# An encoder trunk on one core: gate and up of the FFN by Strassen's scheme, activations kept in memory

## The chip, the cores and the metric

The kernel runs on one core of a Trainium2 chip. The metric is the device time of one execution in microseconds (us), given as the median of three runs; one further execution was profiled, and all rows below come from it. The engines are called PE (TensorE, matmuls), PEld (its weight loads), DVE (VectorE), ACT (ScalarE), POOL (GpSimd) and SP (which issues DMAs).

## What is computed

Two sequences, a prompt of 512 tokens and a sample of 256, go through the same trunk of two layers, width 1024. Each layer is attention with three kinds of heads, then a SwiGLU FFN of width 2816. The change concerns the second half of a layer:

```python
for l in range(DEPTH):
    ...
    x = x + y @ w_out[l]
    h = rms_norm(x, norm_ffn[l])
    gate, up = jnp.split(h @ w_gate_up[l], 2, axis=-1)
    x = x + (jax.nn.silu(gate) * up) @ w_down[l]
```

## The kernel before, in words

**Layout and precision.** Activations lie transposed: 128 of the 1024 features on the partitions in each of `KC` = 8 chunks k, tokens on the free axis. `X[0]` holds the prompt (512 columns), `X[1]` the sample (256). Each fp32 operand is split in two F32R parts, hi (a cast, mostly on ACT) and lo (value minus hi, on DVE or POOL), and each product is three matmuls into the same PSUM bank: hi·hi, hi·lo, lo·hi (`mm3`, L509 to L512). The parts of the normalised activations are `Tph`, `Tpl` (512 columns) and `Tsh`, `Tsl` (256).

**Order.** Nothing is ordered by hand. `Plan` records every operation with a cost, a priority and the buffers it reads and writes, and then lists them one by one: the order on each engine is fixed when the kernel is built, and an engine waits at the head of its list. Buffers belong to kinds ("W", "RAW", "SG", ...), and an operation that needs a buffer of a kind takes the one free first.

**Passage into the FFN.** `emit_out` multiplies the attention output by `w_out` and adds it to `X` (DVE). `norm2` then splits `X` times the norm's gain into the two parts (ACT, then DVE at L544), squares it (L553, L556), splits the sum (L524, L525), adds it over the partitions with a matmul on ones (L530) and takes the reciprocal root as exp(−½ ln) on ACT (L533, L535). The root isn't needed by the matmuls: it scales their results (L1002).

**FFN.** `emit_ffn` goes over the 22 blocks f of 128 FFN columns in parts of 6, 6, 6 and 4 (`FPARTS`). A block's gate and up (u = 0, 1) take, for the prompt and the sample each, 8 chunks × 3 = 24 matmuls, of 512 and of 256 columns: 96 matmuls a block. Its weights are two pieces of 512 KB (`Piece`: DMA into `raw`, cast to `wh` on ACT, difference `wl` on DVE or POOL at L485, L486). Then come the scaling by the root (DVE, L1002), silu (ACT, L1005), gate times up (POOL, L1007), and the two parts of the product (ACT at L1014 and `alo`), which stay in SBUF in buffers of kind "ACT". After the blocks of a part come its 8 output chunks c of the second product, 3 matmuls per block and sequence, added to `X` on DVE. The last part of four blocks goes by 256 tokens.

Of the kernel before, what the change touches and what calls it, by code (L numbers as in the profile page):

```python
# [16 lines left out]
KC = 8  # L17
# [5 lines left out]
FPARTS = (6,6,6,4)  # L23
# [53 lines left out]
class Plan:  # L77
# [4 lines left out]
    FIFO = {"S", "P", "PT", "PTS", "PO", "OT", "OV", "Y", "TB", "BT", "GP", "GS", "W", "RAW", "ACT", "SG", "SQ", "YR", "IV", "YT", "RB", "MC", "CS", "QKG"}  # L82
    GROUP = {"MC": "TB"}
    PSUM = {"D", "S", "PT", "PO", "M", "ANY"}

    def __init__(self):
        self.ops, self.writer, self.readers = [], {}, {}
        self.tiles, self.kinds, self.same, self.unit = [], {}, [], []
        self.floor = -1e9

    def storage(self, kind, bundles):
        lst = self.kinds.setdefault(kind, [])
        for b in bundles:
            ids = []
            for t in b:
# [4 lines left out]
                else:  # L100
                    self.tiles.append(t)
                    ids.append(len(self.tiles) - 1)
                    old = [b for a, b in self.same if a is t]
                    self.unit.append(next(i for i, u in enumerate(self.tiles) if u is old[0]) if old else ids[-1])
            lst.append(tuple(ids))

    def alias(self, new, old):
        for a, b in zip(new, old):
            self.same.append((a, b))
# [42 lines left out]
    def emit(self):  # L152
        clock, dma_free, busy = {}, 0.0, {}
        free = [0.0] * len(self.tiles)
# [19 lines left out]
        def slot_time(o):  # L174
            t, picks, taken = 0.0, [], set()
            for b in o.alloc:
# [3 lines left out]
                for ids in self.kinds[b.kind]:  # L180
                    if any(self.unit[i] in taken for i in ids):
                        continue
                    f = max(free[self.unit[i]] for i in ids)
                    if f < best:
                        best, pick = f, ids
# [3 lines left out]
                taken.update(self.unit[i] for i in pick)  # L189
# [30 lines left out]
        while left:  # L220
# [25 lines left out]
            if o.alloc:  # L246
                for b, ids in zip(o.alloc, slot_time(o)[1]):
# [3 lines left out]
                    for i in ids:  # L251
                        free[self.unit[i]] = INF
# [10 lines left out]
            for b in o.bufs:  # L263
# [4 lines left out]
                if not b.left:  # L268
                    for i in b.slot:
                        free[self.unit[i]] = b.end + self.HOP  # L270
# [15 lines left out]
def trunk(ctx: ExitStack, tc: tile.TileContext, t):  # L286
# [905 lines left out]
```

## Time and profile before

| | us |
|---|---|
| median of three runs | 1836.93 (1836.65 to 1838.26) |
| profiled execution | 1836.76 |
| its span | 1835.0 |
| PE busy | 1792.1 (98%) |
| DVE busy | 934.1 (51%) |
| ACT busy | 765.4 (42%) |
| POOL busy | 479.1 (26%) |

The span is the time between the first and the last instruction of the profiled execution. Busy times of PE come from matmuls that overlap in the pipeline, so the mean duration of one matmul is longer than its distance to the next; distances are read from the timeline.

### The profile page before, as it was taken

The numbers are of one execution on the slowest core, as the hardware profiler recorded it, in microseconds if no ns is written. First come the engines' busy times: TensorE is split into PE (matmuls) and PEld (weight loads), VectorE is DVE, ScalarE is ACT, GpSimd is POOL, SyncE is SP. The second block draws the span as 40 slices with busy tenths as digits, with TensorE's granted clock in tenths as the row PEclk, the third lists the DMA queues.
The fourth block names the chain that finished last, engine by engine and source line by source line (L and its number), as shares of the span: only waits on it lengthen the run. The fifth ranks groups of instructions, "written<-read, shape, count | busy, mean of one in ns | idle before, by whom it ended". The sixth has DMA issues, their size and how long they took to land. (4 is left out here: it accounts for less than half of the span.)

```text
span 1835.0 us, 29851 instructions
## 1 busy us (share of the span) xinstructions
PE 1792.1 (98%) x11984; PEld 1638.9 (89%) x11984; DVE 934.1 (51%) x1835; ACT 765.4 (42%) x1745; POOL 479.1 (26%) x523
## 2 busy tenths in 40 slices
PE   6999999999999999999999999998999999999999
PEld 5999999888888888888999989998888888888889
DVE  7788687762333233333668876768423222222222
ACT  5887586642112112212458756857321221122120
POOL 1564253321101101201215634522230131122031
PEclk9999999999999999999999999999999999999999
DMA  4321110121221222121222202001212112211212
GB/s 154 81 69 36 36 56 26 35 69 50 66 69 55 61 69 69 53 75 58 69 63 71 60 24 65 24 24 36 69 58 80 58 52 71 72 56 54 77 58 81
DMA packets 56891, 110.60 MB, mean 60 GB/s; under 512 B 24496, under 2 KB 29616, under 8 KB 56752
## 3 DMA queue, kind: packets, MB, share of 16 engines
q1 hardware_dynamic: 56752, 108.69, 19.3%
q8 instruction: 94, 1.54, 0.4%
q14 instruction: 45, 0.37, 0.1%
HBM read 105.52 MB, written 3.15 MB: 59 GB/s over the span
## 5 line engine op out<-in xcount | busy, mean ns | idle before, releaser
L485 ACT CAST wh<-raw 128x1024 fp32r<-128x1024 f32 (+1 forms) x186 | 184.4, 992 | 486.1 <-PE ps L511 482.2
L1007 POOL TENSOR_TENSOR p<-p,p 128x512 f32<-128x512 f32 (+1 forms) x88 | 115.0, 1307 | 803.7 <-DVE p L1002 720.7
L486 DVE TENSOR_TENSOR wl<-raw,wh 128x1024 fp32r<-128x1024 f32 (+1 forms) x166 | 194.8, 1174 | 168.5 <-ACT wh L485 168.2
L510 PE MATMUL ps<-Tph,wh 128*128 128x512 f32 x704 | 278.1, 395 | 0.0
L511 PE MATMUL ps<-Tpl,wh 128*128 128x512 f32 x704 | 277.9, 395 | 0.0
L512 PE MATMUL ps<-Tph,wl 128*128 128x512 f32 x704 | 273.9, 389 | 0.0
L511 PE MATMUL ps<-Tsl,wh 128*128 128x256 f32 x704 | 199.1, 283 | 0.0
L512 PE MATMUL ps<-Tsh,wl 128*128 128x256 f32 x704 | 199.2, 283 | 0.0
L510 PE MATMUL ps<-Tsh,wh 128*128 128x256 f32 x704 | 197.5, 281 | 0.0
L1002 DVE TENSOR_TENSOR p<-ps,cs 128x512 f32<-128x512 f32 x88 | 60.4, 686 | 233.6 <-PE ps L512 233.3
L510 PE MATMUL ps<-wh,Tph 128*128 128x256 f32 x512 | 152.7, 298 | 10.0 <-ACT wh L481 8.3
L512 PEld LDWEIGHTS ps<-Tph,wl 128*128 128x128 f32 x704 | 132.4, 188 | 30.1
L511 PE MATMUL ps<-wl,Tph 128*128 128x256 f32 x512 | 147.0, 287 | 5.0 <-DVE wl L482 5.0
L510 PEld LDWEIGHTS ps<-Tph,wh 128*128 128x128 f32 x704 | 133.5, 190 | 17.5
L512 PE MATMUL ps<-wh,Tpl 128*128 128x256 f32 x512 | 147.1, 287 | 0.8 <-DVE Tpl L544 0.8
L511 PEld LDWEIGHTS ps<-Tpl,wh 128*128 128x128 f32 x704 | 133.6, 190 | 15.2
L510 PEld LDWEIGHTS ps<-Tsh,wh 128*128 128x128 f32 x704 | 133.7, 190 | 14.1
L511 PEld LDWEIGHTS ps<-Tsl,wh 128*128 128x128 f32 x704 | 133.7, 190 | 12.8 <-DVE Tsl L544 0.2
L512 PEld LDWEIGHTS ps<-Tsh,wl 128*128 128x128 f32 x704 | 133.7, 190 | 0.0
L510 PE MATMUL ps<-yt,wh 128*128 128x256 f32 (+1 forms) x448 | 132.8, 296 | 0.7 <-DVE xp L963 0.4
L511 PE MATMUL ps<-yt,wh 128*128 128x256 f32 (+1 forms) x448 | 130.6, 291 | 0.0
L512 PE MATMUL ps<-yt,wl 128*128 128x256 f32 (+1 forms) x448 | 130.1, 290 | 0.0
(241 smaller groups left out, 4396.5 us busy)
## 6 DMA issues: line engine op xcount, KB each, us to landing
raw<-in_w_gu SPq DMA_DIRECT2D x88, 512.0 KB, 3.7
raw<-in_w_down SPq DMA_DIRECT2D x48, 384.0 KB, 3.1
raw<-in_w_in SPq DMA_DIRECT2D x32, 512.0 KB, 3.8
raw<-in_w_out SPq DMA_DIRECT2D x16, 512.0 KB, 3.6
raw<-in_w_down SPq DMA_DIRECT2D x8, 512.0 KB, 3.7
tbm<-in_rpb SPq DMA_DIRECT2D x96, 24.0 KB, 2.2
tbm<-in_rpb SPq DMA_DIRECT2D x48, 48.0 KB, 2.4
out_y<-xp SPq DMA_DIRECT2D x8, 256.0 KB, 2.1
```

Of the source, the lines that this page charges most:

```text
L485: act(width, lambda: ACT.copy(self.flat(0), raw[0][:, :width]), r=[raw], w=w[0], prio=prio)
L486: ew(width, lambda E: E.tensor_tensor(self.flat(1), raw[0][:, :width], self.flat(0).bitcast(F32), op=OP.subtract), r=[raw] + w[0], w=w[1], ...
L510: PE.matmul(out, a[0], b[0], start=start, stop=False)
L511: PE.matmul(out, a[0], b[1], start=False, stop=False)
L512: PE.matmul(out, a[1], b[0], start=False, stop=stop)
L1002: dve(n, lambda n=n, u=u, s=s, sg=sg, view=view: DVE.tensor_tensor(sg[u][:, :n], view(u), late[s][0][:, :n], op=OP.mult), r=[accs[u % len( ...
L1007: ew(n, lambda E, n=n, sg=sg: E.tensor_tensor(sg[1][:, :n], sg[0][:, :n], sg[1][:, :n], op=OP.mult), r=[(sg, 0)], w=[(sg, 1), sg], prio=pb ...
```

## The change

**Storage.** All tokens lie in one tile `X` of 768 columns in the order sample, prompt (`OFF`); its halves are the first 384 and the second 384 columns. The parts of the activations, the attention buffers and the new Strassen operands share one large tile `u` of 31 units of 768 columns. Reciprocals in attention take a buffer of another kind, and the squares have one buffer in `norm2`.

**Gate and up.** The activations are seen as a matrix of 2 × 2 blocks: features k < 4 (A) and k ≥ 4 (B) of the first 384 tokens, C and D of the second 384. The weights of a block f are four pieces (256 KB each): features below or above, gate or up. The first `FIRST_F` = 2 blocks of each layer multiply plainly, in matmuls of 384 columns. The other 20 use Strassen's scheme in Winograd's form: seven products of 4 chunks instead of eight, with four sums of weights per block (`sums`) and four sums of activations T1 to T4 per layer, made in `norm2` with their two parts (L646 to L687). Five banks take the results; bank X is added on by three products and copied by ACT after each, and DVE adds the others to the copies.

**Activations through memory.** Gate times up of every block goes to `spill` in DRAM by DMA and is loaded again for the second product, where its two parts are made (`load`). The second product runs behind all 22 blocks, in matmuls of 384 columns, in chunks of 6, 6, 6 and 4 blocks.

```diff
-FPARTS = (6,6,6,4)
+HALF = 384
+OFF = {2: 0, 0: 256, 1: 512}
+NU = 31
+DCH = (6, 6, 6)
+FIRST_F = 2
...
+        def half2(ps, a, z, pr):
...
+            for k in range(4):
...
+                parts(lambda k=k: x(1, k), u["C"], a, z, g0, rx(k), pr)
+                dve(n, lambda D=D, k=k, g1=g1: DVE.tensor_scalar(v(D), x(1, k + 4), g1, None, op0=OP.mult), r=rx(k), w=[D],
+                    prio=pr, fast=True, lock=True, ptr=True)
+                parts(lambda D=D: v(D), u["D"], a, z, None, [D], pr)
+            pr = L + 198.2
+            for k in range(4):
...
+                ew(n, lambda E, E1=E1, k=k: E.tensor_tensor(v(E1), x(1, k), x(0, k), op=OP.subtract), r=rx(k), w=[E1], prio=pr,
+                   on="DVE POOL")
+                dve(n, lambda T2=T2, E1=E1, D=D, g0=g0: DVE.scalar_tensor_tensor(
+                    v(T2), v(E1), g0, v(D), op0=OP.mult, op1=OP.subtract), r=[D, E1, "gcol"], w=[T2], prio=pr, lock=True, ptr=True)
+                parts(lambda T2=T2: v(T2), u["T2"], a, z, None, [T2], pr)
...
+    def sums(srcs, width, prio, after):
...
+        for m, i in (("A11", 0), ("S1", 2), ("A22", 3), ("A12", 1)):
+            dma(128 * 4 * width, lambda m=m, i=i: SP.dma_start(out=raw(m), in_=srcs[i]), w=[q[m]], prio=prio,
+                after=after)
+        for out, x, y, op in (("S3", "S1", "A11", OP.subtract), ("S1", "S1", "A22", OP.add), ("S2", "A11", "S1", OP.subtract),
+                              ("S4", "A12", "S2", OP.add)):
+            ew(width, lambda E, out=out, x=x, y=y, op=op: E.tensor_tensor(raw(out), raw(x), raw(y), op=op), r=[q[x], q[y]],
+               w=[q[out]], prio=prio, on="wadd")
+        for m in b:
+            act(width, lambda m=m: ACT.copy(hi(m), raw(m)), r=[q[m]], w=[(b[m], 0)], prio=prio)
+            ew(width, lambda E, m=m: E.tensor_tensor(lo(m), raw(m), hi(m).bitcast(F32), op=OP.subtract),
+               r=[q[m], (b[m], 0)], w=[(b[m], 1)], prio=prio, on="slo")
...
+    PRODUCTS = (("A11", "A", "X"), ("A12", "B", "Y"), ("S2", "T2", "X"), ("S4", "D", "Z"), ("S3", "T3", "X"), ("A22", "T4", "W"),
+                ("S1", "T1", "V"))
...
+        for f in range(FIRST_F, FC):
+            pr = base + f
+            wb = sums([t["w_gu"][l, f, i] for i in range(4)], 512, pr - 1.5, ends)
...
+            for x, (wn, un, bn) in enumerate(PRODUCTS):
...
+                product(wb[wn], [U[k][un] for k in range(4)], bank[bn], 4, pp, utok, un == "A" or bn != "X", True)
+                pw = pp - 0.05
+                if bn == "X":
+                    i = ("A", "T2", "T3").index(un)
+                    act(HALF, lambda sg=sg, i=i, b=bank["X"]: ACT.copy(sg[i], b[0][:, :HALF]), r=[bank["X"]], w=[(sg, i)],
+                        prio=pw, sbuf=False)
+                else:
+                    for dst, src, op in {"Y": ((0, 0, OP.add),), "Z": ((1, 1, OP.add),), "W": ((3, 2, OP.add),),
+                                         "V": ((1, 1, OP.add), (2, 2, OP.add))}[bn]:
+                        dve(HALF, lambda sg=sg, dst=dst, src=src, op=op, b=bank[bn]: DVE.tensor_tensor(
+                            sg[dst], sg[src], b[0][:, :HALF], op=op), r=[bank[bn], (sg, src)], w=[(sg, dst)], prio=pw)
...
+        def load(f, kind, prio):
...
+                dma(196 << 10, lambda q=q, hs=hs: SP.dma_start(out=q[0][:, :HALF], in_=spill[f][:, hs]), r=[("spill", f, h)],
+                    w=[q], prio=prio)
```

**What it moves.** Three places of layer 0 show the order of before and of the change around the end of norm2; buffers carry their names in the program.

On DVE, where the last split sums of the norm stand (`yt`, the lo part), before:

```order
L556 TENSOR_TENSOR p2_139<-p2_139,p3_140 128x512
L556 TENSOR_TENSOR tbm_144<-tbm_144 128x512
L486 TENSOR_TENSOR wl0_85<-raw0_89,wh0_81 128x1024
L486 TENSOR_TENSOR wl1_86<-raw1_90,wh1_82 128x1024
L553 TENSOR_TENSOR p3_140<-xp_67 128x512
L556 TENSOR_TENSOR p2_139<-p2_139,p3_140 128x512
L525 TENSOR_TENSOR yt2_128<-p0_137,yt2_128 128x256
L525 TENSOR_TENSOR yt1_127<-tbm_144,yt1_127 128x256
L486 TENSOR_TENSOR wl2_87<-raw0_89,wh2_83 128x1024
L525 TENSOR_TENSOR yt0_126<-p2_139,yt0_126 128x256
L486 TENSOR_TENSOR wl3_88<-raw1_90,wh3_84 128x1024
L1002 TENSOR_TENSOR p0_137<-ps3_76,bt0_148 128x256
```

On DVE, the same place in the change (`u` are Strassen operands, `row` the root, `raw`, `ppa` and `w` the first Strassen block's weights):

```order
L649 TENSOR_TENSOR u<-bt,u 128x256
L649 TENSOR_TENSOR u<-p,u 128x256
L652 SCALAR_TENSOR_TENSOR u<-p,gcol,u 128x256
L649 TENSOR_TENSOR u<-bt,u 128x256
L1099 TENSOR_TENSOR y<-ps_77,row 128x384
L561 TENSOR_TENSOR yt<-tbm,yt 128x256
L1099 TENSOR_TENSOR sq<-ps_75,row 128x384
L1099 TENSOR_TENSOR sq<-ps_71,row 128x384
L1099 TENSOR_TENSOR y<-ps_72,row 128x384
L1099 TENSOR_TENSOR y<-ps_74,row 128x384
L1053 TENSOR_TENSOR ppa<-raw 128x512
L1057 TENSOR_TENSOR w<-raw,w 128x512
```

Before, weight lo parts (L486) stand between the norm's operations; now sums of activations stand ahead of the last lo part, and the plain blocks' scalings and the weight sums behind it.

On ACT, where the root and the first silu stand, before:

```order
L524 CAST yt0_126<-p2_139 128x256
L485 CAST wh3_84<-raw1_90 128x1024
L533 ACTIVATE bt0_148<-ps7_80,eps_66 128x256
L535 ACTIVATE bt0_148<-bt0_148 128x256
L533 ACTIVATE cs0_145<-ps7_80,eps_66 128x256
L535 ACTIVATE cs0_145<-cs0_145 128x256
L1005 ACT_TABLE_LOAD
L1005 ACTIVATE p0_137<-p0_137 128x256
L1014 CAST g0b0_96<-p1_138 128x256
```

On ACT in the change:

```order
L560 CAST yt<-tbm 128x256
L569 ACTIVATE row<-ps_78,eps 128x256
L571 ACTIVATE row<-row 128x256
L1082 ACT_TABLE_LOAD
L1082 ACTIVATE y<-y 128x384 x2
L1082 ACTIVATE sq<-sq 128x384
L1082 ACTIVATE y<-y 128x384
L1056 CAST w<-raw 128x512 x2
L1056 CAST w<-ppa 128x512
```

Before, the casts of the weights (L485) stand ahead of the table load of silu; now the root, the table load and the silus of the plain blocks stand ahead of the casts (L1056) of the first Strassen block's weights.

On PE, the last matmul of the norm (L530) before, amid gate and up of the first blocks:

```order
L510 MATMUL ps4_77<-Tph_69,wh3_84 128x512
L511 MATMUL ps4_77<-Tpl_70,wh3_84 128x512
L512 MATMUL ps4_77<-Tph_69,wl3_88 128x512
L530 MATMUL ps7_80<-yt1_127,ones_136 128x256 x2
L510 MATMUL ps5_78<-Tsh_71,wh0_81 128x256
L511 MATMUL ps5_78<-Tsl_72,wh0_81 128x256
L512 MATMUL ps5_78<-Tsh_71,wl0_85 128x256
```

On PE in the change (L566 is the same matmul; `ps3` is the bank of a plain block, `ps5` the first Strassen product's):

```order
L546 MATMUL ps3_74<-u_79,w_80 128x384
L547 MATMUL ps3_74<-u_79,w_80 128x384
L548 MATMUL ps3_74<-u_79,w_80 128x384
L566 MATMUL ps7_78<-yt_81,ones_70 128x256 x2
L546 MATMUL ps5_76<-u_79,w_80 128x384
L547 MATMUL ps5_76<-u_79,w_80 128x384
L548 MATMUL ps5_76<-u_79,w_80 128x384
```

It now stands between the last plain product and the first product of the first Strassen block.

## Rows read from the trace of the kernel before

**Rows 1.** Page, part 1: busy us (share of the span) x instructions, by engine.

```profile
PE 1792.1 (98%) x11984; PEld 1638.9 (89%) x11984; DVE 934.1 (51%) x1835; ACT 765.4 (42%) x1745; POOL 479.1 (26%) x523
```

**Rows 2.** Windows: us from:to, length, busy (x) by engine, PE clock, DMA share, GB/s.

```profile
0.00:26.00 26.00, 9.89 (x40) 8.91 (x40) 21.14 (x46) 17.34 (x37) 5.31 (x6) 1.00 0.64 217
26.00:60.00 34.00, 32.51 (x258) 31.99 (x258) 22.11 (x54) 20.28 (x59) 11.09 (x22) 0.95 0.31 83
360.00:395.00 35.00, 34.53 (x225) 31.52 (x225) 28.76 (x48) 20.86 (x41) 10.73 (x9) 1.00 0.20 61
410.00:900.00 490.00, 490.00 (x2837) 431.30 (x2837) 161.66 (x236) 103.86 (x149) 62.28 (x45) 1.00 0.21 64
1262.00:1300.00 38.00, 37.98 (x260) 35.20 (x259) 33.17 (x64) 22.56 (x45) 2.30 (x3) 1.00 0.13 43
```

**Rows 3.** Waits of PE in 360 to 395: us in total, times, longest.

```profile
PE ps L510 <- DVE xp L963: 0.4, 1, 0.4
```

**Rows 4.** Timeline of PE in the second product: start, duration, engine, line, operation.

```profile
699.96 0.40 PE L510 MATMUL ps<-Tph,wh 128*128 128x512 f32 x1
...
701.35 0.28 PE L510 MATMUL ps<-Tsh,wh 128*128 128x256 f32 x1
...
702.06 0.40 PE L510 MATMUL ps<-Tph,wh 128*128 128x512 f32 x1
```

**Rows 5.** Timeline of ACT, the gate's silus of two blocks.

```profile
425.92 0.94 ACT L1005 ACTIVATE p<-p 128x256 f32<-128x256 f32 x2
...
442.76 0.94 ACT L1005 ACTIVATE p<-p 128x256 f32<-128x256 f32 x2
```

**Rows 6.** Timeline of DVE in the passage of layer 0.

```profile
361.02 1.69 DVE L544 SCALAR_TENSOR_TENSOR Tpl<-xp,gcol,Tph 128x256 fp32r<-128x256 f32 x4
...
365.66 0.41 DVE L939 TENSOR_TENSOR yt<-y,yt 128x256 fp32r<-128x256 f32 x1
365.99 1.27 DVE L544 SCALAR_TENSOR_TENSOR Tpl<-xp,gcol,Tph 128x256 fp32r<-128x256 f32 x3
...
377.52 0.68 DVE L553 TENSOR_TENSOR p<-xp 128x512 f32<-128x512 f32 x1
378.12 0.68 DVE L553 TENSOR_TENSOR tbm<-xs 128x512 f32<-128x512 f32 x1
```

**Rows 7.** DVE by form: operation x count | busy, mean ns | idle before.

```profile
L674 DVE TENSOR_TENSOR ppa<-ps,qkg 128x384 f32<-128x384 f32 x48 | 26.4, 550 | 5.3 <-ACT ppa L673 5.0
...
L859 DVE TENSOR_TENSOR rp<-ps,rp 128x128 fp32r<-128x128 f32 x24 | 6.8, 281 | 0.3 <-ACT rp L858 0.2
```

**Rows 8.** ACT by form, same columns.

```profile
L1014 ACT CAST g0a<-p 128x512 fp32r<-128x512 f32 x18 | 11.1, 618 | 92.2 <-POOL p L1007 92.2
...
L715 ACT CAST stk<-ppa 128x384 fp32r<-128x384 f32 x48 | 24.5, 510 | 19.0 <-PE ps L728 6.6 <-DVE ppa L710 6.4 <-POOL ppa L710 5.2
...
L533 ACT ACTIVATE rb<-ps,eps 128x256 f32<-128x256 f32 x18 | 8.5, 474 | 4.5 <-PE ps L530 2.5 <-PE ps L519 1.8
L535 ACT ACTIVATE rb<-rb 128x256 f32<-128x256 f32 x18 | 7.5, 418 | 0.3
...
L1005 ACT ACT_TABLE_LOAD x2 | 2.6, 1283 | 0.0
```

**Rows 9.** POOL by form, same columns.

```profile
L716 POOL TENSOR_TENSOR stk<-ppa,stk 128x384 fp32r<-128x384 f32 x16 | 16.3, 1016 | 21.6 <-ACT stk L715 21.6
...
L1007 POOL TENSOR_TENSOR p<-p,p 128x256 f32<-128x256 f32 x44 | 58.2, 1322 | 271.2 <-DVE p L1002 201.4 <-ACT p L1005 69.8
L1007 POOL TENSOR_TENSOR p<-p,p 128x512 f32<-128x512 f32 x44 | 56.9, 1293 | 532.5 <-DVE p L1002 519.3 <-ACT wh L485 13.2
...
L906 POOL TENSOR_TENSOR yr<-y 128x256 f32<-128x256 f32 x30 | 22.1, 738 | 52.0 <-DVE y L903 52.0
```

**Rows 10.** DMA issues: operation x count, KB each, us to landing.

```profile
raw<-in_w_gu SPq DMA_DIRECT2D x88, 512.0 KB, 3.7
...
out_y<-xp SPq DMA_DIRECT2D x8, 256.0 KB, 2.1
```

More of the change, by code (lines that the diff above doesn't have):

```diff
@@ L102, in storage, with atom, part, named @@
                     ids.append(len(self.tiles) - 1)
-                    old = [b for a, b in self.same if a is t]
-                    self.unit.append(next(i for i, u in enumerate(self.tiles) if u is old[0]) if old else ids[-1])
+                    at = [a for z, a in self.same if z is t]
+                    self.unit.append(at[0] if at else (self.atom(None, 0),))
             lst.append(tuple(ids))
-    def alias(self, new, old):
-        for a, b in zip(new, old):
-            self.same.append((a, b))
+    def atom(self, key, i):
+        if key is None or (key, i) not in self.grid:
+            self.natoms += 1
+            if key is None:
+                return self.natoms - 1
+            self.grid[key, i] = self.natoms - 1
+        return self.grid[key, i]
+    def part(self, whole, key, lo, hi):
+        t = whole[:, lo:hi]
+        return self.named(t, key, lo, hi)
+    def named(self, t, key, lo, hi):
+        self.same.append((t, tuple(self.atom(key, i) for i in range(lo // 128, -(-hi // 128)))))
+        return t
     def buf(self, kind):
@@ L180, in slot_time @@
                 for ids in self.kinds[b.kind]:
[L181 removed]
+                    if taken and any(z in taken for i in ids for z in unit[i]):
                         continue
[L183 removed]
+                    f = max([free[z] for i in ids for z in unit[i]])
                     if f < best:
@@ L251, in emit @@
                     for i in ids:
-                        free[self.unit[i]] = INF
+                        for z in unit[i]:
+                            free[z] = INF
             o.start = s
@@ L269, in emit @@
                     for i in b.slot:
-                        free[self.unit[i]] = b.end + self.HOP
+                        for z in unit[i]:
+                            free[z] = b.end + self.HOP
             for z in o.opts:
@@ L920, in emit_out @@
             q = sq[m, p]
-            late = K["lo"] and m == TURN[-1]
-            rb = P.buf("RBL" if late else "RB")
+            rb = P.buf("RB")
             root([(lambda q=q: q[0], q)], wd, po, K["om"] if m == TURN[-1] else 0, rb, lambda rb=rb: rb[0], rb)
@@ new lines, in trunk, with product, mm @@
+    PRODUCTS = (("A11", "A", "X"), ("A12", "B", "Y"), ("S2", "T2", "X"), ("S4", "D", "Z"), ("S3", "T3", "X"), ("A22", "T4", "W"),
+                ("S1", "T1", "V"))
+    def product(wb, ub, bank, n, prio, tok, first, last, open_=True):
+        for kk in range(0, n, 2):
+            ks = list(range(kk, min(kk + 2, n)))
+            def mm(ks=ks):
+                for k in ks:
+                    w = [wb[0][:, z * 512 + k * 128:z * 512 + k * 128 + 128] for z in range(2)]
+                    u = [ub[k][0][:, z * HALF:z * HALF + HALF] for z in range(2)]
+                    mm3(bank[0][:, :HALF], w, u, first and k == 0, last and k == n - 1, open_ and not first)
+            pe(3 * len(ks) * (HALF / 2400.0 + 0.014), mm, r=[(wb, 0), (wb, 1)] + [x for k in ks for x in tok(ub[k])], w=[bank], prio=prio)
@@ L1094, in trunk @@
         P.floor = L + 90
-        ends, late = norm2(l, [L + K["nf"] + p + (K["n2"] if p == 2 else 0.0) for p in range(3)])
+        ends, row, U = norm2(l, [L + K["nf"] + p + (K["n2"] if p == 2 else 0.0) for p in range(3)])
         P.floor = -1e9
-        last = emit_ffn(l, L + 200, ends, late)
+        last = emit_ffn(l, L + 200, ends, row, U)
         if l + 1 < DEPTH:
```

525 lines of the change are left out of this document (268 added, 257 removed).

## The prediction

> **What bounds the kernel now.** I read the shares of busy time first, then stretches of the span, then TensorE's own rows, then the rows that price the work of the other engines. TensorE is busy 98% of the span, VectorE 51%, ScalarE 42%, GpSimd 26% [rows 1]. The reader should see in the stretches that this is not an average over good and bad: in 490 us of FFN TensorE stands 0.00 us and VectorE works a third of the time [rows 2]. So the FFN's time is its matmul columns. The places where TensorE does wait are the first 26 us (9.89 busy [rows 2]) and bits of attention; 1835.0 − 1792.1 [rows 1] leaves 42.9 us of waiting, 16.1 of it in those 26 us. The passage from attention to the FFN, which the change rewrites, is nearly free of waits today: 0.47 us stand in 35 in layer 0, with one wait of 0.4, and 0.02 in 38 in layer 1 [rows 2, 3]. But VectorE is the engine that works hardest there, 28.76 of 35 and 33.17 of 38 [rows 2].
>
> My sum starts from the profiled execution, 1836.76 us, 0.2 us under the median of the three runs. No change can be told from a change under 0.2%, about 3.7 us.
>
> **Price of the matmuls.** Six 512-column matmuls start within 1.39 us (699.96 to 701.35), six 256-column ones within 0.71 (to 702.06) [rows 4]: 0.2317 and 0.1183 each. A block of 128 FFN columns has 48 of either: 48 × 0.35 = 16.8 us. Two silus of neighbouring blocks start 425.92 and 442.76, 16.84 apart, which agrees [rows 5]. The change's 384-column matmul isn't in the trace. 512 + 256 columns cost 0.35, so two of 384 cost the same if time goes by columns: 0.175. Scaled from the narrow row alone it would be 1.5 × 0.1183 = 0.1775, from the wide one 0.75 × 0.2317 = 0.1738. I take 0.175, since the pair holds the same columns, and keep those bounds.
>
> **Strassen blocks.** Seven products × 4 contraction chunks × 3 = 84 matmuls of 384, 84 × 0.175 = 14.7 us against 16.8. Saved: 2.1 us in each of 20 blocks in each of 2 layers, **−84**. By the bounds of the price it is 40 × (16.8 − 14.91) = −76 to 40 × (16.8 − 14.6) = −88. The two plain blocks of a layer have 192 matmuls of 384, 33.6 us, as before. The second product has the same columns (3 × 0.2317 + 3 × 0.1183 = 1.05 before, 6 × 0.175 = 1.05 after, per FFN block and output chunk), and its last part stays: 0.
>
> **The passage into the FFN.** The new norm2 makes, besides the two parts of the scaled activations, four Strassen sums of them and their two parts, and VectorE does most of it. By the order of the changed program in layer 0, from VectorE's row of the first add of the sample's attention output (L1026) to the last lo part of the root (L561, the excerpt), there stand 28 operations of 512 columns between tensors, 31 scalar-tensor ones of 256 and 28 of 128, 27 tensor-tensor ones of 256 and 16 of 128, 8 tensor-scalar ones and 4 of 384 out of PSUM. Prices, start to start: 0.60 for 512 (377.52 to 378.12), (1.69 − 0.08)/4 = 0.40 for a scalar-tensor one of 256, 0.33 for a tensor-tensor one of 256 (365.66 to 365.99) [rows 6]; 0.47 for 384 out of PSUM (550 ns less the overlap of 0.08) and 0.20 for 128 (281 less the same) [rows 7]. The scalar-tensor one of 128 and the tensor-scalar ones aren't shown: the first lies between 0.20 (the tensor-tensor one of 128) and 0.40 (its own of 256), I take 0.26 and so −1.7 to +3.9 us on the stretch; for the second 0.2 to 0.3. Sum: 16.8 + 12.4 + 7.3 + 9.0 + 3.2 + 1.9 + 1.9 = 52.5 us. TensorE's rows in the same stretch are 108 matmuls of 256 (12.8 us), the 192 of the plain blocks (33.6) and the roots' (0.9): 47.3. VectorE is **5.2 us late**, and nothing later on TensorE's queue is free of it: in the excerpt of TensorE the last root matmul stands between the last plain product and the first Strassen product. Before, it stood amid gate and up products, with 512-column work on both sides.
>
> Behind that root there is a chain. The root's Ln and Exp (0.47 and 0.42), the load of silu's table (1.28), four silus of 384 (about 0.42 each by the 0.51 of a 384 cast less overlap), and only then on ScalarE's queue the casts of the first Strassen weights (0.54 start to start, from 0.62), and VectorE's lo part (0.60) [rows 6, 8]: the excerpt of ScalarE shows this order. With the root's matmuls (0.3) that is 5.3 us in which TensorE's next product has no weights. Before, the casts of the weight pieces stand ahead of the table load in ScalarE's order. So layer 0 stands 5.2 + 5.3, about **11 us**. In layer 1 the stretch has 33 operations of 512, three more of 256 and four more of 384: 58.5 us against 12.8 + 204 × 0.175 + 0.9 = 49.4 up to the product that first needs the last of them: **9 us**. Both could be zero if GpSimd and ScalarE take the work sooner than I count, and both could be 15 if VectorE must wait for ScalarE's hi parts ahead of each lo part.
>
> **The clock after a gap.** After the first 26 us, in which TensorE was busy 38%, the next 34 us ran at a mean granted clock of 0.95, everywhere else in the FFN at 1.00 [rows 2]. 0.95 of 34 is 1.7 us lost, that is 3.4 us at 1.2 GHz. Two gaps of about 10 us may each bring that: **+3**, between 0 and 3.4. By the Trainium skill ("TensorE: Matmul & The Clock Gate", "What's actually happening") the array's default is the throttled state, half rate, and activity releases it; the row agrees, and by the rule the two gaps cost as much as by the row if they are unbroken, nothing if scattered.
>
> **Steady Strassen blocks.** Per block of 14.7 us VectorE has 4 sums of weights and 6.1 of 7 lo parts at 0.60, 5 reads of PSUM at 0.47 and 3.1 scalings at 0.5: 9.9 us. ScalarE has 7 casts (0.62) and 5 other operations of 384 (0.51): 6.9. GpSimd has 2.2 products and 0.9 scalings of 384 (1.02 each) and 0.9 lo parts of 512 (1.29): 4.3 [rows 6 to 9]. All are below 14.7, so they hide behind TensorE. Weights and banks are awaited 80 to 100 matmuls after the work that frees them stands in order; the closest is the bank that three products add on, whose copy by ScalarE has 10 matmuls, 1.75 us, of cover, against a copy of 0.5 behind at most one cast of 0.62. I take **+1** for all blocks, with 0 and 24 (0.6 a block) as ends. Transfers: four of 256 KB a block and two spills replace two of 512 KB (3.7 us each) [rows 10]; the second product's reloads stand 18 to 27 matmuls (3 to 5 us) ahead. At a DMA share of 0.21 [rows 2] I cost them at nothing; uncovered, a reload is about 2.1 us (a 256 KB store [rows 10]).
>
> **Storage.** One buffer fewer in attention (reciprocals shared, squares single) and weights in other places: 0, between −3 and +3, a tenth of the 26.8 us that TensorE waits outside the start.
>
> Sum: 1836.8 − 84 + 11 + 9 + 3 + 1 = 1776.8, so **1777 us**.
>
> **Rivals.**
> *The passage is covered.* The row for it: before, TensorE waits 0.4 us there with VectorE at 82% [rows 2, 3], and two plain blocks give 33.6 us of cover. Against it: the counts above. Time: 1836.8 − 84 + 0 to 4 = 1753 to 1757.
> *The blocks are bound in part.* Each block stands 0.25 to 0.6 us at the shared bank or at a late lo part: 40 of them cost 10 to 24, so 1787 to 1801. For it: scalings and lo parts are queued in order on VectorE among PSUM reads; against it: the 5 us of slack.
> *The other side: VectorE and GpSimd lengthen each other until a block is theirs.* GpSimd's 256-column product takes 1322 ns among VectorE's work, another 256-column operation of its, in attention, 738 [rows 9]. If not one of their operations could overlap, a block would take 9.9 + 4.3 = 14.2, still under 14.7. It decides from a block of 14.7 + (84 − 24)/40 = 16.2, when each operation is also 14% longer than its row; a block of 16.8 would give 1837 + 24 = about 1861. The Trainium skill ("SBUF — State Buffer", "Who interferes with whom") says that a VectorE operation with two inputs in SBUF and a GpSimd operation that reads SBUF hold a shared pair of ports exclusively. By that rule only 7.6 + 4.3 = 11.9 us of a block exclude each other, which is no bound either; the two rows agree that the engines hinder each other.
>
> **How the numbers follow.** Forecast 0.66, passage covered 0.12, blocks bound in part 0.14, other side 0.08. The forecast's own bounds (76 to 88 saved, stalls 10 to 28, clock 0 to 3, storage ±3) give 1756 to 1796 with all at one end; taking in most of the first two rivals makes 1753 to 1804. Faster 0.89 (all but the last case and a little for the unforeseen), same 0.03, slower 0.08.
>
> **What would show it.** Right: silus of neighbouring Strassen blocks 14.7 us apart; TensorE free of waits in the blocks; a gap of about 10 us in each layer ahead of the first Strassen product, released by VectorE or by the weights' cast; a granted clock under 1 just behind it. Wrong: 384-column matmuls far from 0.175 us, which moves the sum by 1 us for each 0.0003; blocks of 15.3 or more, with waits for ScalarE's bank copies; passages without a gap; GpSimd rows much longer than 1.3 us.

## The result, and the profile after

The changed kernel takes 1783.11 us (median of four, 1781.19 to 1784.08) against 1837.56 for the kernel before: a ratio of 0.9703, 95% interval 0.9686 to 0.9719, so 54.5 us less. The forecast was 1777, its range 1753 to 1804. The profiled execution has a span of 1782.3 us, 52.7 less than that of before.

The shares of busy time of the changed kernel, to be read beside [rows 1]:

```profile
PE 1712.3 (96%) x11504; PEld 1682.5 (94%) x11504; DVE 1310.0 (74%) x2511; ACT 917.7 (51%) x2151; POOL 542.0 (30%) x577
```

TensorE lost 79.8 us of busy time, but its share fell: 1782.3 − 1712.3 leaves 70.0 us of waiting, 27.1 more than before. VectorE went from 934.1 to 1310.0 us.

ScalarE's timeline in the Strassen blocks of the changed kernel, the first silu of a block and the first of the next, which answer to [rows 5]:

```profile
601.85 0.53 ACT L1082 ACTIVATE y<-y 128x384 f32<-128x384 f32 x1 [1.28 <-DVE y L1127]
...
616.40 0.53 ACT L1082 ACTIVATE y<-y 128x384 f32<-128x384 f32 x1 [1.28 <-DVE y L1127]
```

A block takes 616.40 − 601.85 = 14.55 us (five blocks from there take 72.80, 14.56 each), against 16.8: a 384-column matmul is 14.56 / 84 = 0.1733 us.

TensorE's waits in the changed kernel over the whole span (us in total, times, longest), some of the rows that answer to [rows 3]; layer 0's waits in front of the Strassen blocks follow piece by piece below:

```profile
PE ps L548 <- DVE w L1057: 9.7, 2, 9.4
...
PE ps L956 <- DVE y L971: 4.2, 2, 2.1
...
PE ps L546 <- DVE x L1026: 3.8, 4, 1.0
...
PE ps L546 <- ACT y L1115: 0.8, 1, 0.8
```

and four of its stretches, with the columns of [rows 2]:

```profile
350.00:400.00 50.00, 46.82 (x310) 46.12 (x311) 45.12 (x115) 30.15 (x81) 14.19 (x17) 0.97 0.05 17
395.00:411.20 16.20, 15.89 (x91) 15.26 (x89) 16.16 (x46) 9.16 (x25) 2.48 (x2) 1.00 0.00 2
400.00:430.00 30.00, 21.17 (x99) 19.43 (x98) 27.15 (x54) 16.29 (x34) 7.78 (x6) 0.77 0.24 82
430.00:800.00 370.00, 369.22 (x2129) 368.69 (x2129) 282.15 (x426) 152.73 (x285) 103.61 (x81) 1.00 0.36 111
```

The reader sees two gaps: in layer 0, 21.17 of 30 us busy at a mean clock of 0.77; then blocks that wait for 0.78 us in 370. Ahead of the gap it is VectorE that is full: 16.16 of 16.2 us, where ScalarE is busy 9.16. In layer 1 there is one wait of 9.4 for the lo part of a weight (L1057). TensorE's timeline shows the gap of layer 0 piece by piece:

```profile
413.90 0.58 PE L566 MATMUL ps<-yt,ones 128*128 128x256 f32 x1 [3.00 <-ACT yt L560]
415.36 0.58 PE L566 MATMUL ps<-yt,ones 128*128 128x256 f32 x1 [0.88 <-DVE yt L561]
420.54 0.69 PE L546 MATMUL ps<-u,w 128*128 128x384 f32 x1 [4.59 <-ACT w L1056]
...
421.90 0.69 PE L548 MATMUL ps<-u,w 128*128 128x384 f32 x1 [0.36 <-DVE w L1057]
```

3.00 and 0.88 us are lost ahead of the two last root matmuls, 4.59 and 0.36 ahead of the first Strassen weights: 8.8 us.

### The profile page after: what moved, and what is told of

Same layout as the page of the kernel before. It is cut to its first block, busy times and chain, and to the rows that moved or that the text cites. A ratio compares the mean times of both kernels' runs of the same rounds, so it can differ in the third digit from the quotient of the medians.

```text
span 1782.3 us, 30961 instructions
## 1 busy us (share of the span) xinstructions
PE 1712.3 (96%) x11504; PEld 1682.5 (94%) x11504; DVE 1310.0 (74%) x2511; ACT 917.7 (51%) x2151; POOL 542.0 (30%) x577
## 4 chain that ended last, share of the span: by engine, by line
PE 81%; DVE 10%; ACT 7%; issue 1%; DMA 1%; SPq 0%; DVEq 0%
PE ps L546 24%; PE ps L547 24%; PE ps L548 24%; PE ps L956 3%; PE ps L934 2%; PE ps L875 2%; ACT p L922 1%; ACT u L941 1%; DVE u L652 1%; ACT w L521 1%; DVE w L522 1%; PE ps L807 1%; DVE u L649 1%; DVE x L1026 1%; DVE u L942 1%
## 5 line engine op out<-in xcount | busy, mean ns | idle before, releaser
L548 PE MATMUL ps<-u,w 128*128 128x384 f32 (+1 forms) x1684 | 559.7, 332 | 9.7 <-DVE w L1057 9.7
L546 PE MATMUL ps<-u,w 128*128 128x384 f32 (+1 forms) x1684 | 559.8, 332 | 5.4 <-ACT w L1056 4.6
L547 PE MATMUL ps<-u,w 128*128 128x384 f32 (+1 forms) x1684 | 559.3, 332 | 0.0
L548 PEld LDWEIGHTS ps<-u,w 128*128 128x128 f32 x1684 | 317.8, 189 | 10.6 <-DVE w L1057 10.6
L546 PEld LDWEIGHTS ps<-u,w 128*128 128x128 f32 x1684 | 317.7, 189 | 6.5 <-ACT w L1056 4.9
L547 PEld LDWEIGHTS ps<-u,w 128*128 128x128 f32 x1684 | 317.8, 189 | 0.0
L546 PE MATMUL ps<-w,u 128*128 128x256 f32 x768 | 228.8, 298 | 12.5 <-ACT w L521 9.3
L547 PE MATMUL ps<-w,u 128*128 128x256 f32 x768 | 219.1, 285 | 5.3 <-DVE w L522 5.3
L548 PE MATMUL ps<-w,u 128*128 128x256 f32 x768 | 219.2, 285 | 0.0
L521 ACT CAST w<-raw 128x1024 fp32r<-128x1024 f32 (+2 forms) x102 | 94.9, 932 | 209.2 <-PE ps L547 187.8
L546 PEld LDWEIGHTS ps<-w,u 128*128 128x128 f32 x768 | 148.6, 193 | 14.6 <-ACT w L521 9.3
L547 PEld LDWEIGHTS ps<-w,u 128*128 128x128 f32 x768 | 148.9, 194 | 6.3 <-DVE w L522 5.6
L548 PEld LDWEIGHTS ps<-w,u 128*128 128x128 f32 x768 | 148.5, 193 | 0.0
L546 PE MATMUL ps<-yt,w 128*128 128x256 f32 x392 | 114.3, 291 | 3.9 <-DVE x L1026 3.8
L522 DVE TENSOR_TENSOR w<-raw,w 128x768 fp32r<-128x768 f32 (+2 forms) x87 | 97.2, 1119 | 24.8 <-ACT w L521 17.8
L956 PE MATMUL ps<-u 128*128 128x256 f32 (+1 forms) x592 | 105.6, 296 | 9.4 <-DVE u L942 4.6
L547 PE MATMUL ps<-yt,w 128*128 128x256 f32 x392 | 111.9, 286 | 0.2 <-DVE yt L1012 0.2
L548 PE MATMUL ps<-yt,w 128*128 128x256 f32 x392 | 111.6, 285 | 0.0
L942 DVE TENSOR_TENSOR u<-ps,u 128x512 fp32r<-128x512 f32 (+1 forms) x160 | 97.2, 625 | 18.2 <-ACT u L941 17.4
L875 PE MATMUL ps<-u 128*128 128x256 f32 (+1 forms) x384 | 94.8, 349 | 7.8 <-DVE sm L919 3.9
L956 PEld LDWEIGHTS ps<-u 128*128 128x128 f32 x592 | 84.7, 194 | 14.6 <-DVE u L942 7.1
```

The costliest lines, as they stand in the source:

```text
L521: act(n, lambda hs=hs: ACT.copy(self.flat(0)[:, hs], raw[0][:, hs]), r=[raw], w=[(b, 0) + z], prio=prio)
L522: ew(n, lambda E, hs=hs: E.tensor_tensor(self.flat(1)[:, hs], raw[0][:, hs], self.flat(0)[:, hs].bitcast(F32), op=OP.subtract), r=[raw, (b ...
L546: PE.matmul(out, a[0], b[0], start=start, stop=False, skip_group_check=on)
L547: PE.matmul(out, a[0], b[1], start=False, stop=False, skip_group_check=on)
L548: PE.matmul(out, a[1], b[0], start=False, stop=stop, skip_group_check=on)
L875: PE.matmul(S[0][:, :nk], q, kk[:, k0:k0 + nk], start=i == 0, stop=i == 1)
```

## The experiments

Each time is a median with its ratio to the kernel before on the same chip, and its interval.

**One more plain block per layer.**

```diff
-FIRST_F = 2
+FIRST_F = 3
...
-        for h in range(2):
-            for f in range(FIRST_F):
-                sg, pp = sgs[f], base - 1 + 0.4 * h + 0.2 * f
+        for h, f in [(0, 0), (0, 1), (1, 0), (1, 1)] + [(h, f) for f in range(2, FIRST_F) for h in range(2)]:
+            if True:
+                sg, pp = sgs[f], base - 1 + 0.4 * h + 0.2 * f + (0.8 if f > 1 else 0.0)
```

> A third plain block per layer ahead of the Strassen blocks, nothing else. Theory (the two gaps of 8.9 and 9.4 us are VectorE's and ScalarE's lateness after the sums of activations, with 5.5 us of half clock behind them): 16.6 us more cover closes both, so -18.3 - 5.5 + 2 x (16.64 - 14.56) = about -19.6, 1763 us, and no gap. Rival chain (root, table load, silus and the casts of the first Strassen weights hang together wherever the first Strassen block stands): the 5 us of layer 0 stay, behind the third block, and layer 1's may too: 1770 to 1787. Rival banks (the third block's own weights come late, since its casts queue behind norm2's): a new wait ahead of the third block, 1775 or more.

Measured: 1771.53 us, 0.9636 (0.9621 to 0.9650), 11.6 us less than the changed kernel. TensorE's two longest waits of this kernel from 380 to 440 us, in layer 0:

```profile
PE ps L546 <- DVE y L1099: 3.6, 1, 3.6
PE ps L546 <- ACT y L1115: 2.0, 1, 2.0
```

And its waits from 1250 to 1330 us, in layer 1:

```profile
PE ps L546 <- DVE y L1099: 1.6, 1, 1.6
PE ps L546 <- ACT y L1115: 1.4, 1, 1.4
```

Both gaps for weights are gone, also the 4.6 us behind the root, so the chain was not tied to the Strassen block: it only had no cover. In their place stand waits that no theory named: the third block's accumulators need banks, and a bank is held until VectorE has scaled it by the root (L1099), which is still late; and the first Strassen blocks wait for ScalarE's copy of bank X (L1115). They are 3.6 + 2.0 + 1.6 + 1.4 = 8.6 us, about what is missing between the 11.6 us that came back and 19.6. By its time alone the run would fit the chain rival's 1770 to 1787; the waits which that rival needs are gone.

**The sums of activations left out.**

```diff
             pr = L + 198.2
-            for k in range(4):
+            for k in range(0):
                 u, D = U[k], Ds[k]
...
-                product(wb[wn], [U[k][un] for k in range(4)], bank[bn], 4, pp, utok, un == "A" or bn != "X", True)
+                product(wb[wn], [U[k][{"T1": "B", "T2": "C", "T3": "D", "T4": "A"}.get(un, un)] for k in range(4)], bank[bn], 4, pp, utok, un == "A" or bn != "X", True)
```

> The sums of activations T1 to T4 aren't made; their products take B, C, D, A in their place, so the matmuls stay and norm2 loses about 19 us of VectorE work a layer. Theory: layer 1's gap of 9.4 goes, layer 0's shrinks by at least the 3.9 us ahead of the root, and the clock's 5.5 with them: 1760 to 1767. Rival chain: the gaps stay where the casts of the first Strassen weights are late: 1778 to 1783.

Measured: 1766.18 us, 0.9606 (0.9592 to 0.9620). In layer 0's passage these waits are left, besides one of 0.2 us:

```profile
PE ps L546 <- DVE x L1026: 1.9, 2, 1.0
PE ps L548 <- DVE w L1057: 0.3, 1, 0.3
```

Without the sums the gaps are 0.3 us. The chain of root, table load, silus and casts is still there, in the same form, and costs nothing when it starts earlier; the rival falls. The sums also gave ScalarE and GpSimd work, so this run alone doesn't say which engine was late; the row from 395 to 411.2 us does, where VectorE is full and ScalarE isn't. The gaps are VectorE's lateness.

**All blocks plain.**

```diff
-FIRST_F = 2
+FIRST_F = 22
...
```

> All 22 blocks plain (no Strassen product, no sums), with everything else of the change: one tile of tokens, 384 columns, activations through memory, the second product behind all blocks. Theory (these cost nothing, and 20 blocks by Strassen save 2.08 us each against plain ones of 16.64): 1783 + 40 x 2.08 - 18.3 (gaps) - 5.5 (clock) - 3.8 (bank waits of the output product) = 1838.6, the time of the kernel before. Rival (the storage and the way through memory cost something that the Strassen blocks hide in my account): 1845 or more.

Measured: 1842.15 us, 1.0023 (1.0013 to 1.0033), 3.5 us over the sum, under the rival's 1845. The first silus of two blocks are 16.64 us apart:

```profile
507.42 0.53 ACT L1082 ACTIVATE y<-y 128x384 f32<-128x384 f32 x1 [0.15 <-DVE y L1099]
...
524.06 0.53 ACT L1082 ACTIVATE sq<-sq 128x384 f32<-128x384 f32 x1 [0.16 <-DVE sq L1099]
```

So the rest of the change is dearer than the plain kernel by some 4 us, though 384 columns save 0.16 us a block. The Strassen blocks are worth 1842.15 − 1783.11 = 59.0 us, of 40 × 2.08 = 83.2: 24 us were given back, 19 of them in the two gaps and the waits behind them. TensorE's waits for L971 and L1026 stand in this kernel too, 4.4 and 3.8 us, so they belong to the rest of the change and not to the Strassen blocks.

**Matmuls without use in the gaps, twice.** The first run put layer 1's in the wrong place; the second moved them. In the diff the last two lines are the second run against the first.

```diff
...
+                for _ in range(warm if ks[0] == 0 else 0):
+                    PE.matmul(bank[0][:, :HALF], ones, ub[0][0][:, :HALF], start=True, stop=True)
...
-                        warm=(22, 46)[l] if (f, x) == (FIRST_F, 0) else 0)
+                        warm=(24, 46)[l] if (f, x) == (FIRST_F, l) else 0)
```

> Matmuls without use fill the gaps: 32 of 128 columns ahead of layer 0's last root matmul, 22 of 384 behind it, 46 of 384 ahead of the first Strassen product in layer 1. Theory: the gaps end when they ended before, but the clock stays at 2.4 GHz in and behind them, which gives back the 6.6 and 4.4 us at half rate behind the gaps, 5.5 us in all: 1777.6, granted clock 1.00 in the 20 us after each gap. Rival (what runs slowly behind the gap is the late weights, not the clock): 1783, no change.

> As the run before with matmuls without use, but in layer 1 they stand where the gap is (46 ahead of the second product of the first Strassen block), 24 and 32 in layer 0 as before. Theory: both gaps end where they ended, the clock stays at 2.4 GHz behind both: 1783 - 5.5 = 1777.6. If the first run's 1785.8 was right for another reason than the misplaced 46 (8 us ahead of the gap), this one is no faster either: 1783 to 1786.

Measured: 1785.76 us, 0.9715 (0.9699 to 0.9730), with 4.8 us of layer 1's gap left; and 1781.70, 0.9694 (0.9679 to 0.9708). Windows of the changed kernel in and behind the two gaps (PE busy first, the clock third from the end):

```profile
412.00:416.00 4.00, 1.16 (x2) 0.58 (x2) 3.31 (x9) 1.65 (x6) 0.00 (x0) 0.65 0.00 0
416.00:420.00 4.00, 0.00 (x0) 0.00 (x0) 2.55 (x5) 3.94 (x8) 1.19 (x1) 0.50 0.00 0
420.00:424.00 4.00, 3.11 (x9) 2.60 (x10) 3.45 (x3) 0.73 (x2) 4.00 (x4) 0.50 0.61 193
424.00:428.00 4.00, 4.00 (x17) 4.00 (x17) 3.89 (x7) 3.45 (x7) 0.11 (x1) 0.65 0.68 229
1300.00:1304.00 4.00, 1.11 (x3) 1.11 (x4) 3.96 (x9) 1.57 (x4) 0.00 (x0) 0.50 0.16 57
1304.00:1308.00 4.00, 4.00 (x15) 4.00 (x15) 4.00 (x8) 3.31 (x7) 0.00 (x0) 0.57 0.54 161
```

and of the second run:

```profile
416.00:420.00 4.00, 3.56 (x21) 3.56 (x22) 2.57 (x7) 3.07 (x6) 0.29 (x1) 1.00 0.00 0
420.00:424.00 4.00, 2.83 (x15) 2.19 (x15) 2.96 (x3) 1.38 (x4) 4.00 (x4) 1.00 0.44 93
424.00:428.00 4.00, 3.19 (x16) 2.34 (x15) 3.88 (x6) 2.79 (x6) 1.04 (x1) 1.00 0.77 252
1300.00:1304.00 4.00, 2.58 (x15) 2.26 (x14) 3.96 (x8) 1.48 (x4) 0.00 (x0) 1.00 0.07 25
1304.00:1308.00 4.00, 4.00 (x24) 3.85 (x24) 4.00 (x7) 2.90 (x6) 0.00 (x0) 1.00 0.84 234
```

The clock does follow the gap: filled, it stays at 2.4 GHz, where the changed kernel runs behind both gaps at 1.2 GHz. The windows give the rate lost in the changed kernel as the clock below 1 times TensorE's busy time: 0.4 + 1.6 + 1.4 in layer 0 and 0.6 + 1.7 in layer 1, some 5.6 us. But the medians are only 1.4 us apart, which is within the spread of the runs. In the traces 1.1 us came back in layer 0 (from the last plain matmul to a silu deep in the blocks, 410.56 to 616.40 us against 411.64 to 616.36) and 1.3 in layer 1 (from its first silu, 1282.05 to 1493.93 against 1281.14 to 1491.73).

Behind layer 0's gap TensorE is busy 3.19 of 4 us instead of 4.00: at full rate it stands still for operands that aren't ready. One is a weight whose cast waits for its load (ScalarE's timeline of the second run):

```profile
424.85 0.62 ACT L1059 CAST w<-raw 128x512 fp32r<-128x512 f32 x1 [3.47 <-DMA raw<-in_w_gu]
```

In the changed kernel that load is issued at 420.79 us, right behind the first spill in SyncE's queue; the spill waits 30.4 us for GpSimd's product, and so for the root. Behind layer 1's gap TensorE is busy 4.00 us in both, and does 24 matmuls instead of 15. So the clock cost less than its lost rate, 1.4 us by the medians and 2.4 by the traces, in layer 0 since the engine that it slowed would have waited.

**A buffer of its own for attention's reciprocals.**

```diff
...
-            inv, iv = P.buf("M"), P.buf("YR")
+            inv, iv = P.buf("M"), P.buf("IV")
```

> The reciprocals of attention get a buffer of their own again (64 more columns in the row's tile). The change's attention has 5.7 us more waits and 4.7 us more half clock than before. Theory that the shared buffer makes them: they go, 1773 to 1777. Rival (they come from the new order, VectorE taking norm2's work for the sample ahead of attention's last adds): 1781 to 1785.

Measured: 1786.03 us, 0.9718 (0.9703 to 0.9732). TensorE's waits for L971 and L1026 fell from 8.0 to 4.5 us, but all its waiting is 70 us as before: others took their place. So a buffer of its own gave no time back; whether the shared one has a part in those waits isn't settled.

**VectorE's slack in a block.** S4, one of the four sums of weights, is computed 5, 10 and 2 times.

```diff
-            ew(width, lambda E, out=out, x=x, y=y, op=op: E.tensor_tensor(raw(out), raw(x), raw(y), op=op), r=[q[x], q[y]],
+            ew(width, lambda E, out=out, x=x, y=y, op=op: [E.tensor_tensor(raw(out), raw(x), raw(y), op=op)
+                                                                for _ in range(5 if out == "S4" else 1)], r=[q[x], q[y]],
```

> In each Strassen block one sum of weights (S4) is computed five times instead of once, with the same result: 2.4 us more VectorE work a block, order unchanged. VectorE is busy 282 of 370 us in the blocks of layer 0, 11.1 us of 14.56. Theory (blocks are TensorE's until VectorE fills them): 13.5 of 14.56, so only the first block of each layer is later, +2 to +5: 1785 to 1788. Rival (blocks are bound in part already, VectorE's queue in order): 0.5 us or more a block, 1803 or more.

> The same sum ten times: 5.4 us more VectorE work a block. Theory: 11.1 + 5.4 = 16.5 us of VectorE in a block of 14.56, VectorE becomes the bound: 40 x 1.9 = +78, 1855 to 1870, slower than the kernel before; the slack of a block lies between the two runs. Rival (VectorE's busy time holds waits that shrink): under 1830.

> S4 computed twice instead of once in each Strassen block, same result, order unchanged: one more VectorE operation of 512, 0.6 to 0.9 us a block. The run with four more lost 2.84 us a block though VectorE was not full. Theory now: VectorE's queue holds the row scaling, the silu waits for it at the head of ScalarE's queue, and the copy of the shared bank X stands behind the silu; the block has about the 2.2 us of slack in which VectorE is idle in the changed kernel, so one operation fits: 1783 to 1787. Rival (no slack at all, each operation costs its 0.7 us a block): 1808 to 1813.

Measured: 1896.68 us, 1.0312 (1.0295 to 1.0329); 2090.28, 1.1372 (1.1355 to 1.1389); 1788.48, 0.9732 (0.9716 to 0.9748). My theory of the first two fell: four more operations cost 113.6 us, 2.84 a block, while VectorE isn't full. The window 500 to 700 us of the changed kernel:

```profile
500.00:700.00 200.00, 200.00 (x1156) 200.00 (x1155) 164.34 (x242) 87.84 (x168) 70.05 (x54) 1.00 0.35 103
```

The same window with S4 computed 2 times:

```profile
500.00:700.00 200.00, 200.00 (x1156) 200.00 (x1155) 173.28 (x259) 85.09 (x169) 71.49 (x55) 1.00 0.35 103
```

Four steady blocks with S4 computed 5 times:

```profile
612.72:680.25 67.53, 59.36 (x336) 58.08 (x336) 61.22 (x89) 24.53 (x49) 20.95 (x17) 1.00 0.29 86
```

And 10 times, from 500 to 700 us:

```profile
500.00:700.00 200.00, 146.01 (x726) 143.13 (x725) 168.82 (x248) 53.55 (x105) 46.61 (x34) 0.85 0.22 66
```

The expectations had the added work too small: one of the sums takes 0.91 us there (4.56 for five, below), not 0.60. With four more, VectorE is busy 61.22 / 4 = 15.3 us a block, against 164.34 / 200 × 14.56 = 12.0 in the changed kernel. That is over 14.56, but by VectorE alone a block would be 15.3; it is 67.53 / 4 = 16.88, and VectorE is idle for 1.6 of it. With nine more it is idle for 31 of 200 us.

The run of 5 times shows why, first in VectorE's timeline:

```profile
606.15 4.56 DVE L1053 TENSOR_TENSOR raw<-tbm,ppa 128x512 f32<-128x512 f32 x5
610.63 1.48 DVE L1121 TENSOR_TENSOR y<-y,ps 128x384 f32<-128x384 f32 x3
612.02 1.94 DVE L1128 TENSOR_TENSOR y<-y,row 128x384 f32<-128x384 f32 x2
```

In ScalarE's at the same time:

```profile
612.72 0.52 ACT L1083 ACTIVATE y<-y 128x384 f32<-128x384 f32 x1 [5.24 <-DVE y L1128]
613.15 0.60 ACT L1057 CAST w<-p 128x512 fp32r<-128x512 f32 x1
613.66 0.47 ACT L1116 COPY y<-ps 128x384 f32<-128x384 f32 x1
```

And in TensorE's:

```profile
614.18 0.45 PE L546 MATMUL ps<-u,w 128*128 128x384 f32 x1 [2.04 <-ACT y L1116]
```

The five sums take 4.56 us; the PSUM reads and the row scaling (L1128) wait behind them; the silu waits 5.24 us for the scaling at the head of ScalarE's queue (1.28 in the changed kernel); the copy of the shared bank X (L1116) stands behind it and a cast; and TensorE waits 2.04 us for that copy in every one of these blocks. With one more operation the steady blocks don't change (TensorE 200.00 of 200 busy); the kernel is 5.4 us longer, of which waits for bank X in the first blocks of each layer, up from 0.8 to 4.6 us, are most. The slack of a block is thus between the 0.65 us that VectorE's load rose here (173.28 − 164.34 in 200 us) and the 3.3 of the run with four more.

**GpSimd's FFN work on VectorE.**

These are the entries that change in both layers' settings:

```diff
...
-     slo='POOL DVE', rg='DVE POOL', ru='POOL DVE',
+     slo='DVE', rg='DVE', ru='DVE',
...
-     gu2='POOL',
+     gu2='DVE',
...
```

> VectorE takes what GpSimd did in the FFN blocks: gate times up, the row scalings, the lo parts of the weights; by the rows of before 2 x 0.47 + 0.9 x 0.47 + 0.9 x 0.60 = 1.9 us a block more. VectorE was put at 9.9 us a block and measured at 12.0. Theory (the 2.1 us between are VectorE operations stretched while GpSimd works): VectorE alone needs 9.9 + 1.9 = 11.8 us, as much as now, and the time stays, 1780 to 1790, with rows of 0.68 and 0.55 only. Rival (GpSimd's share was a net relief): VectorE at 13.9 us, and by the loads tried before 40 us or more: 1820 and up.

Measured: 1786.44 us, 0.9720 (0.9706 to 0.9734). The same window of this kernel:

```profile
500.00:700.00 200.00, 200.00 (x1155) 200.00 (x1155) 168.20 (x301) 88.00 (x172) 1.33 (x1) 1.00 0.35 103
```

VectorE's operations in it by form, in the changed kernel:

```profile
L1120 DVE TENSOR_TENSOR y<-y,ps 128x384 f32<-128x384 f32 x55 | 28.8, 545 | 0.5 <-ACT y L1115 0.4
L1127 DVE TENSOR_TENSOR y<-y,row 128x384 f32<-128x384 f32 x35 | 24.8, 727 | 0.0
...
L1057 DVE TENSOR_TENSOR w<-ppa,w 128x512 fp32r<-128x512 f32 x17 | 16.5, 973 | 0.8 <-ACT w L1056 0.8
```

GpSimd's costliest form there:

```profile
L1083 POOL TENSOR_TENSOR y<-y,sq 128x384 f32<-128x384 f32 x14 | 18.5, 1337 | 0.5
```

VectorE's forms with GpSimd silent:

```profile
L1120 DVE TENSOR_TENSOR y<-y,ps 128x384 f32<-128x384 f32 x55 | 29.6, 547 | 0.3 <-ACT y L1115 0.3
L1127 DVE TENSOR_TENSOR y<-y,row 128x384 f32<-128x384 f32 x42 | 22.7, 553 | 0.5
...
L1057 DVE TENSOR_TENSOR w<-ppa,w 128x512 fp32r<-128x512 f32 x13 | 8.9, 685 | 1.2 <-ACT w L1056 1.2
```

With 59 more instructions VectorE is busy only 3.9 us longer. The 54 operations of GpSimd in these 200 us (41 of 384 columns, 13 of 512) would by my estimate take VectorE 32, at 0.553 and 0.685 each. So some 28 us of its time had been stretching: GpSimd's help cost VectorE nearly as much as it took off it. VectorE's operations with two inputs in SBUF shrink from 727 to 553 and from 973 to 685 ns when GpSimd is silent, those that read PSUM stay at 545 and 547.

**Two steps further, and the last output product's banks.** The kernel with three plain blocks, with the lo parts of the sums on VectorE alone; and the changed kernel with other banks for the product ahead of norm2.

```diff
...
-nlo2='DVE POOL'
+nlo2='DVE'
...
```

```diff
-                acc = P.buf("D")
+                acc = P.buf("ANY" if m == TURN[-1] else "D")
```

> The kernel with three plain blocks, and the lo parts of the sums of activations on VectorE alone instead of VectorE or GpSimd. Theory: in the passage GpSimd's operations stretch VectorE's as in the blocks, so VectorE ends earlier by 1 to 3 us a layer: 1766 to 1771. Rival (GpSimd took work off the late engine): 1772 to 1780.

> The changed kernel, but the last output product ahead of norm2 may take any free PSUM bank instead of two of its own. Its four waits of 0.9 to 1.0 us for VectorE's adds (the adds stand behind six operations of norm2 in VectorE's order) are 3.8 us in all. Theory: the waits go, and the matmuls behind them stand closer ahead of VectorE's lateness, so the gaps in front of the Strassen blocks grow by as much: 1782 to 1785. Rival (the waits add to the gaps): 1779 or less.

Measured: 1768.44 us, 0.9622 (0.9608 to 0.9637), the fastest kernel of the study that leaves nothing out, though its interval overlaps that of three plain blocks alone, so a gain from the lo parts isn't shown; and 1782.49, 0.9699 (0.9683 to 0.9715). In the second the four bank waits, 3.8 us, are gone and the time is the changed kernel's within the spread. The waits in front of the Strassen blocks grew, but not by as much: 10.6 us against 9.7 in layer 0, 9.7 against 9.4 in layer 1. So some of the time won ahead of VectorE's lateness is lost in front of it; where the rest went wasn't settled.

## Why the prediction was right, point by point

**The bound.** Right: TensorE's columns set the FFN, and the blocks run without waits.

**The matmul.** 0.175 was 0.1733, just under the lower bound of 0.1738. The saving of the 40 blocks was 89.6 us by 14.56 a block, not 84, and over the forecast's own end of 88: mis-sized by 5.6.

**The passage.** 11 and 9 us were forecast; 8.8 and 9.4 were measured. In layer 0 the parts were 3.9 ahead of the root's matmuls (5.2 forecast) and 5.0 behind it (5.3). The mechanism, VectorE's lateness with a chain behind it, held in the run without sums and in the run with more cover. The sizes agree in part by luck. VectorE's stretch in layer 0 runs from the first to the second of these rows:

```profile
358.67 1.28 DVE L1026 TENSOR_TENSOR x<-ps,x 128x512 f32<-128x512 f32 x2
...
414.90 0.41 DVE L561 TENSOR_TENSOR yt<-tbm,yt 128x256 fp32r<-128x256 f32 x1
```

That is 56.6 us where 52.5 was counted (27 × 0.33 is 8.9 there, not 9.0), and TensorE came to the end of the last plain product at 410.9, 52.2 us behind the same start, where 47.3 was counted with the roots. Each count was 4 to 5 us too short, and the lateness is their difference.

**The clock.** 3 us were forecast from the row after the first 26 us. 5.6 us of rate were lost behind the gaps (3.4 and 2.3 in the windows above). Filling the gaps gave back 1.4 by the medians and 2.4 by the traces, so about that much was the clock's own price there: the mechanism is right, the lost rate was nearly twice the term, and part of it was time in which TensorE would have waited anyway.

**Steady blocks.** 0.8 us of waits in layer 0's (1 forecast). But VectorE's load in a block, put at 9.9, was 12.0, and GpSimd's, put at 4.3, was 70.05 / 200 × 14.56 = 5.1. The step that failed is the prices of single operations under "All are below 14.7, so they hide behind TensorE"; what it concluded held, with less room than counted. By the estimate above GpSimd's neighbourhood stretches VectorE's operations by some 2 us a block, nearly what the same work would take on VectorE. The Trainium skill ("SBUF — State Buffer", "Who interferes with whom") says that a VectorE operation with two SBUF inputs and a GpSimd operation reading SBUF exclude each other; the forms above agree, and so does the unchanged PSUM read.

**The rival on the other side** had its point of decision wrong. I asked for VectorE and GpSimd in full succession and each operation 14% longer, a block of 16.2 us. With four more sums VectorE had 15.3 us to do in a block, less than that, and the kernel was 3% slower than before, since the copy that TensorE needs stands behind a silu that waits for VectorE. It is not the sum of an engine's work alone that decides, and the margin was thinner than the rival's 0.08 was worked out from. The two rows from which the engines were said to hinder each other (1322 and 738 ns) are also not of the same operation: one multiplies two tiles, the other squares one. The run with GpSimd silent shows the hindrance, on VectorE's side.

**Storage.** Forecast 0, ±3; this term failed, though not shown to be by the storage itself. TensorE waits 4.2 us for VectorE's adds of the heads (L971) and 3.8 for the output's adds (L1026); [rows 2] had 0.47 us of waiting from 360 to 395. Here is VectorE's timeline around the second:

```profile
362.62 1.27 DVE L1026 TENSOR_TENSOR x<-ps,x 128x512 f32<-128x512 f32 x2
363.82 2.45 DVE L652 SCALAR_TENSOR_TENSOR u<-x,gcol,u 128x256 fp32r<-128x256 f32 x6
366.19 0.68 DVE L591 TENSOR_TENSOR tbm<-x 128x512 f32<-128x512 f32 x1
366.80 1.27 DVE L1026 TENSOR_TENSOR x<-ps,x 128x512 f32<-128x512 f32 x2
```

Six operations of norm2 (L652) and a square (L591) stand between two pairs of adds, and the product has two banks. A buffer of its own for the reciprocals took some of these waits away and gave no time back. Why L971 comes late was not settled. Around such waits the clock falls too: 0.97 in 350 to 400 us, where the kernel before has 1.00. Over windows of 4 us, the clock below 1 times TensorE's busy time is 4.6 us more outside the passages than before, nearly all in attention, which no term had.

**The sum**, by what was measured. Waiting rose by 27.1 us: 18.2 at the passage, 0.8 in the blocks, 8.0 elsewhere, nearly all in attention. Busy time fell by 79.8: 89.6 for the blocks and 288 × 0.01 + 4 × 0.16 = 3.5 for second products (18 blocks, 8 chunks, 2 layers, three pairs of matmuls each) and plain blocks of 384 columns, less 5.6 and 4.6 of clock, make 82.9; 3.1 us are not assigned. The profiled execution, 1784.08, lies 7.3 above the sum: attention's waits and clock, 12.6, taken as nothing, the clock behind the gaps 2.6 too small and the 3.1, against a saving taken 9 too small and passage and blocks 2 too large. Two misses larger than the error stand against each other, so that the number came this close is partly luck.

## What to carry to other kernels

A cut in TensorE's work is worth what its neighbours' queues allow: the passage into the cheaper blocks gave back a fifth of the gain, because the operands of the cheaper scheme have to be made first, and a third plain block as cover returned 11.6 us. Slack isn't only the idle share of an engine: follow each queue from the operation that would grow to the instruction that TensorE waits for, and ask what stands in front of it there. Work handed to GpSimd beside a busy VectorE is not off VectorE's bill, where the operations of both have two inputs in SBUF, as here.

## What the runs showed that I had not expected

What GpSimd did in 70 us of a window of 200 could be put on VectorE for 3.9 us more busy time. A fall of the granted clock from 2.4 to 1.2 GHz behind gaps of 9 us cost 1.4 us in two layers by the medians, 2.4 by the traces, where 5.6 of rate were lost. And a load of weights that stands behind a spill in SyncE's queue waits with it for the root.
